# Forgetting attention with a dense MLP on one Trainium2 core: the weights' scale moves into the exponential's bias, and GpSimd takes the low parts of the first 512 keys

## The chip, the core and the metric

The kernel runs on one core of one Trainium2 chip. A core has five engines that work through queues of their own: TensorE (PE, matrix products; PEld is its weight load), VectorE (DVE), ScalarE (ACT), GpSimd (POOL) and SyncE (SP, which here only issues DMAs). The metric is the device time of one execution in microseconds; less is better.

## The reference, cut to what matters

One layer (`DEPTH = 1`): forgetting attention over 2048 frames with 16 heads of 64, then an MLP of width 4096.

```python
def fox_mixer(h, w_in, b_f, q_g, k_g, w_out):
    proj = h @ w_in
    q, k, v, f_pre = jnp.split(proj, [D, 2 * D, 3 * D], axis=-1)
    ...
    F = jnp.cumsum(log_f, axis=1).transpose(0, 2, 1)
    ...
        logits = (jnp.einsum('bqhd,bkhd->bhqk', q_i, k).astype(jnp.float32) * scale
                  + (F_i[..., :, None] - F[..., None, :]))
        logits = jnp.where(k_pos[None, :] <= q_pos[:, None], logits, -jnp.inf)
        p = jax.nn.softmax(logits, axis=-1).astype(v.dtype)
        return jnp.einsum('bhqk,bkhd->bqhd', p, v)
    ...
    return o @ w_out
```

The layer is `x = x + g_m * fox_mixer(h)` and then `x = x + g_f * (square(relu(h2 @ w_mlp_in)) @ w_mlp_out)`, with normed and shifted `h` and `h2`.

## The kernel before

Precision comes from pairs: a number is split into a high part in a short type and a low part, and products are summed over the pairs. Heads are taken two at a time, as 8 groups `g`. For a group, `sweeps` makes q, k and v of all frames (PE matmuls at L487 to L489 into `psq`, inputs split by ACT into `hh` at L406 and by GpSimd into `hl` at L407). The sweep of the next group is interleaved with `attention` of this one. Attention walks over 16 query blocks `i` of 128 rows, and in each over two heads `h`; what follows calls one (g, i, h) a head. There are 256 heads, and a head of block `i` has W = 128(i+1) keys.

For a head, in this order:

- `att_scores`: PE writes the logits into PSUM, 1024 keys at a time (`S`, two buffers, L537 to L540). One DVE instruction (L544) adds the forget term, writes `L` to SBUF and puts the row maximum of these 1024 keys into `mx`. L549 takes the larger of the one or two maxima and negates it into `st`.
- `att_exp`: ACT turns `L` into exp(L + st) in place, in fp32 (L555). Then, for each chunk of up to `PW` = 1024 keys, ACT writes the fp16 high part of 2^15 times `L` into the first half of a tile `ph` (L562). There are `NPH` = 4 tiles `ph`. Tiles of the same ring also hold `wa` (a weight block that DVE accumulates at L197 while groups 0 to 4 run) and `wv`.
- `att_transpose`: DVE writes the low part, 2^15 `L` minus the high part, into the second half of `ph` (L574). In the last group and from block 8 on, the last 256 keys of a chunk over 512 go to GpSimd, in two instructions (L578 scales, L579 subtracts). Then SP issues a DMA that transposes the whole `ph` into a tile `pT` (L582). There are `NPT` = 5 tiles `pT`.
- `att_values`: PE multiplies the transposed high and low parts with v (L600, L601) into `po`; DVE sums and GpSimd scales the output (L609, L611).

The calls are staggered: `att_transpose` of a head comes after the scores of the next, `att_values` two or three heads later. A scheduler then orders each engine's instructions, and a tile of a ring is taken again when its last reader is done, so a copy L562 can wait for a transpose four chunks back, and a transpose for the values five chunks back. SP runs its queue in order: transposes, loads of `hl` (L403), of `F` (L395), of weights, and stores. After attention comes the output projection with the MLP, which PE fills alone.

Of the kernel before, what the change touches and what calls it, by code (L numbers as in the profile page):

```python
# [4 lines left out]

# [1 line left out]

# [7 lines left out]
F32 = mybir.dt.float32  # L15
# [9 lines left out]
P = 128  # L25
# [12 lines left out]
EPS = 1e-6  # L38
MASK = -1.0e30
PSCALE = 32768.0  # L40
PW = 1024
NL, NPH, NPT, NK, NV, NQD = 3, 4, 5, 6, 7, 1
AHEAD, LEAD, LAG_S, LAG_L = 1, 0.7, 3, 2
# [6 lines left out]
NEARLY, EARLY0 = 5, 12  # L50
TAPER, LEAD1 = 6.6, 0.6
QSH, QDM = 0, 0
LEAD0, NORM_AT, ADA0, ADA1, NF = 0.5, 8, 60, 10, 5


# [2 lines left out]
def fox_layer(ctx, tc, x, c, norm_mix, norm_mlp, w_ada, b_ada, w_mlp_in, w_mlp_out,  # L58
# [77 lines left out]
    def pri(n):  # L136
        return tc.high_priority(offset=n)
# [37 lines left out]
    with ExitStack() as st:  # L175
# [161 lines left out]
        def value_scale(g):  # L337

            wv = sb.tile([P, KB, P], F32, tag="ph" if g else "k", name=f"wv{g}", bufs=NPH if g else NK)
            nc.sync.dma_start(wv, w_in[:, 2 * D + g * P:2 * D + (g + 1) * P].rearrange("(k p) c -> p k c", p=P))  # L340
            r = sb.tile([P, 2], F32, tag="lsr", name=f"lsr_w{g}", bufs=2)
            nc.scalar.activation(wv, wv, AF.Square, accum_out=r[:, 0:1])
            lw = sb.tile([P, 2], F32, tag="lw", name=f"lw{g}", bufs=2)
            log_sum(r, lw, f"w{g}")
            nc.vector.tensor_tensor(lw, lw, hs2, op=ALU.add)
            nc.scalar.activation(vsc[:, g:g + 1], lw[:, 0:1], AF.Exp, scale=-0.5)
            nc.vector.tensor_scalar(vsc[:, g:g + 1], vsc[:, g:g + 1], PSCALE, None, op0=ALU.mult)
            nc.vector.reciprocal(osc[:, g:g + 1], vsc[:, g:g + 1])
            nc.vector.tensor_scalar(osc[:, g:g + 1], osc[:, g:g + 1], 1.0 / PSCALE, None, op0=ALU.mult)

        kT, qT, vT, Fb = {}, {}, {}, {}
        carry = sb.tile([NH, 1], F32, tag="carry", name="carry", bufs=1)
# [169 lines left out]
        def att_scores(g, i, h, st, L):  # L522
# [6 lines left out]
            for cch in range(j + 1):  # L529
# [11 lines left out]
                if last or cch % 2 == 1:  # L541
                    c0, c1 = cch // 2 * 2 * TJ, cch * TJ + w
                    with pri(PR_T):
                        nc.vector.tensor_tensor_reduce(  # L544
                            out=L[:, c0:c1], in0=s2[:, :c1 - c0], in1=Fb[g, h, cch // 2][:, :c1 - c0],
                            scale=1.0, scalar=-3.0e38, op0=ALU.add, op1=ALU.max, accum_out=mx[:, cch // 2:cch // 2 + 1])
                yield
            with pri(PR_T):
                nc.vector.tensor_reduce(out=st[:, h:h + 1], in_=mx[:, :j // 2 + 1], axis=AX.X, op=ALU.max, negate=True)  # L549

        def att_exp(g, i, h, st, L):

# [12 lines left out]

        def att_transpose(g, i, h, L, phs):
            W = (i + 1) * P
            pts = []
            for n, ph in enumerate(phs):
                s0 = n * PW  # L570
                w = min(PW, W - s0)
                c = w - min(w, POOL_B * P) if i >= POOL_I and g >= POOL_G and w > TJ else w
                with pri(PR_PL):
# [7 lines left out]
                with pri(PR_DT):  # L581
                    nc.sync.dma_start_transpose(pT[:, :2 * w // P, :], ph[:, :2 * w])  # L582
                pts.append(pT)
            return pts

        po_of, n_po = {}, [0]
        po_all = psO.tile([P, 2, 2, P], F32, tag="O", name="po")
# [1 line left out]
        def att_values(g, i, h, st, pts):  # L589
# [4 lines left out]
            po = po_of[g, i]  # L594
            for b in range(nb):
                v = vT[g, b // RB][:, b % RB, h, :]
                pT, bb = pts[b * P // PW], b % (PW // P)
                nw = min(PW // P, nb - b + bb)
                with pri(PR_PO):
                    nc.tensor.matmul(po[:, h, :], lhsT=pT[:, bb, :], rhs=v, start=(b == 0), stop=False)  # L600
                    nc.tensor.matmul(po[:, h, 0:HD], lhsT=pT[:, nw + bb, :], rhs=v[:, 0:HD],  # L601
                                     start=False, stop=(b == nb - 1))
                if b % RB == RB - 1:
                    yield
# [342 lines left out]
```

## Time and profile before

| | |
|---|---|
| median of 3 runs | 3117.88 us (3115.86 to 3118.42) |
| the profiled execution | 3121.49 us, of which its instructions span 3119.8 us |
| busy over the span | PE 92%, PEld 76%, DVE 62%, ACT 46%, GpSimd 33% |
| mean granted TensorE clock | 0.966 |

Busy time is a share of the whole span. Attention takes the first 1490 us or so and the MLP the rest, and the shares of the two differ much; the rows below take them apart. An instruction's duration on DVE and GpSimd includes time in which it is held up after it has started.

### The profile page before, as it was taken

The numbers are of one execution on the slowest core, as the hardware profiler recorded it, in microseconds if no ns is written. First come the engines' busy times: TensorE is split into PE (matmuls) and PEld (weight loads), VectorE is DVE, ScalarE is ACT, GpSimd is POOL, SyncE is SP. The second block draws the span as 40 slices with busy tenths as digits, with TensorE's granted clock in tenths as the row PEclk, the third lists the DMA queues.
The fourth block names the chain that finished last, engine by engine and source line by source line (L and its number), as shares of the span: only waits on it lengthen the run. The fifth ranks groups of instructions, "written<-read, shape, count | busy, mean of one in ns | idle before, by whom it ended". The sixth has DMA issues, their size and how long they took to land.

```text
span 3119.8 us, 44614 instructions
## 1 busy us (share of the span) xinstructions
PE 2870.4 (92%) x16587; PEld 2375.9 (76%) x16587; DVE 1930.7 (62%) x3319; ACT 1433.1 (46%) x2267; POOL 1040.5 (33%) x811
## 2 busy tenths in 40 slices
PE   4788889888988898988999999999999999999999
PEld 4667777777877777776788888788887888878887
DVE  6688978988888877878356433443335333453334
ACT  4466766666676767766233322232222223222321
POOL 3354545545464645445332100410013001311103
PEclk9799989999999999998999999999999999999999
DMA  8479999999999989979755432543235323352332
GB/s 274 124 174 208 208 193 218 209 204 208 213 209 211 201 191 197 189 163 211 215 191 200 132 93 80 172 138 95 75 108 203 94 81 108 95 192 91 108 94 69
DMA packets 852122, 502.34 MB, mean 161 GB/s; under 512 B 585396, under 2 KB 782076, under 8 KB 851904
## 3 DMA queue, kind: packets, MB, share of 16 engines
q1 hardware_dynamic: 843536, 469.60, 62.1%
q0 software_dynamic: 8368, 29.89, 2.5%
q8 instruction: 130, 2.13, 0.3%
q14 instruction: 88, 0.72, 0.1%
HBM read 310.50 MB, written 46.28 MB: 114 GB/s over the span
## 4 chain that ended last, share of the span: by engine, by line
PE 49%; DVE 1%; DMA 1%; ACT 0%; issue 0%; SPq 0%; POOL 0%; DVEq 0%; ACTq 0%
PE my L134 8%; PE my L132 7%; PE my L133 7%; PE pu L134 7%; PE pu L132 7%; PE pu L133 7%; PE py L132 1%; PE py L133 1%; PE py L134 1%; DVE w L865 1%; DMA w1r<-in_w_mlp_in_dram 1%; PE xt L799 0%; PE e_py L132 0%; DMA pT<-ph 0%; PE e_py L134 0%; PE e_py L133 0%
## 5 line engine op out<-in xcount | busy, mean ns | idle before, releaser
L574 DVE SCALAR_TENSOR_TENSOR ph<-L,ph 128x1024 f16<-128x1024 f32 (+7 forms) x384 | 438.3, 1152 | 81.2 <-ACT ph L562 79.5
L887 POOL TENSOR_TENSOR rl<-rl 128x512 f32<-128x512 f32 x128 | 139.1, 1086 | 1024.6 <-ACT rl L886 1019.7
L864 ACT CAST w<-w1r 128x1024 fp32r<-128x1024 f32 x128 | 133.5, 1043 | 598.6 <-PE my L134 553.5
L132 PE MATMUL my<-w,a 128*128 128x512 f32 x1024 | 405.0, 396 | 0.1
L133 PE MATMUL my<-w,a 128*128 128x512 f32 x1024 | 402.9, 394 | 0.0
L134 PE MATMUL my<-w,a 128*128 128x512 f32 x1024 | 395.9, 396 | 2.9 <-DVE a L890 2.9
L562 ACT ACTIVATE ph<-L 128x1024 f16<-128x1024 f32 (+7 forms) x384 | 301.7, 804 | 177.4 <-DMA pT<-ph 152.6
L407 POOL TENSOR_TENSOR hl<-hl,hh 128x1024 fp32r<-128x1024 f32 x120 | 299.5, 2497 | 243.7 <-ACT hh L406 205.4
L487 PE MATMUL psq<-w,hh 128*128 128x384 f32 (+1 forms) x960 | 343.5, 359 | 26.5 <-DVE v L496 12.5
L489 PE MATMUL psq<-w,hl 128*128 128x384 f32 (+1 forms) x960 | 354.4, 371 | 3.2 <-POOL hl L407 2.9
L544 DVE CUSTOM_DVE_ANT_0 L<-S,F 128x1024 f32<-128x1024 f32 (+7 forms) x384 | 343.1, 904 | 19.5 <-PE S L538 6.7
L488 PE MATMUL psq<-w,hh 128*128 128x384 f32 (+1 forms) x960 | 342.7, 359 | 6.1 <-POOL w L333 6.1
L555 ACT ACTIVATE L<-L,st 128x128 f32<-128x128 f32 (+15 forms) x256 | 306.7, 1198 | 89.2 <-DVE st L549 84.9
L537 PE MATMUL S<-kT,qT 128*128 128x512 f32 (+3 forms) x640 | 261.8, 411 | 77.4 <-DVE mx L544 66.6
L600 PE MATMUL po<-v,pT 128*128 128x128 f16 x2176 | 277.1, 228 | 55.4 <-DMA pT<-ph 47.0
L865 DVE TENSOR_TENSOR w<-w1r,w 128x1024 fp32r<-128x1024 f32 x128 | 169.9, 1328 | 236.6 <-ACT w L864 236.6
L915 DVE TENSOR_TENSOR ya<-my,ya 128x512 f32<-128x512 f32 x192 | 128.0, 687 | 292.7 <-PE my L134 292.7
L134 PE MATMUL pu<-m_h,w 128*128 128x512 f32 x768 | 304.4, 396 | 0.0
L132 PE MATMUL pu<-m_h,w 128*128 128x512 f32 x768 | 303.8, 396 | 0.0
L133 PE MATMUL pu<-m_h,w 128*128 128x512 f32 x768 | 301.8, 393 | 0.0
L865 DVE TENSOR_TENSOR w<-w2r,w 128x1024 fp32r<-128x1024 f32 x128 | 165.7, 1295 | 203.7 <-ACT w L864 203.7
L600 PEld LDWEIGHTS <-pT 128*128 128x128 f16 x2176 | 205.1, 103 | 86.2 <-DMA pT<-ph 58.3
(214 smaller groups left out, 6115.8 us busy)
## 6 DMA issues: line engine op xcount, KB each, us to landing
w1r<-in_w_mlp_in_dram SPq DMA_DIRECT2D x128, 512.0 KB
w2r<-in_w_mlp_out_dram SPq DMA_DIRECT2D x128, 512.0 KB
hl<-hT_d SPq DMA_DIRECT2D x120, 512.0 KB
F<-nF_d SPq DMA_DIRECT2D x64, 256.0 KB
wa<-in_w_ada_dram SPq DMA_DIRECT2D x32, 512.0 KB
x<-in_x_dram SPq DMA_DIRECT2D x27, 512.0 KB
wr<-in_fox_w_in_dram SPq DMA_DIRECT2D x64, 192.0 KB
h_d<-h2r POOLq DMA_DIRECT2D x24, 512.0 KB, 3.4
```

Source lines behind the costliest of these rows:

```text
L132: nc.tensor.matmul(ps, lhsT=a[0], rhs=b[0], start=first, stop=False)
L133: nc.tensor.matmul(ps, lhsT=a[0], rhs=b[1], start=False, stop=False)
L134: nc.tensor.matmul(ps, lhsT=a[1], rhs=b[0], start=False, stop=last)
L487: nc.tensor.matmul(ps[:, :n], lhsT=hh, rhs=w[:, 0, :n], start=(kb == 0), stop=False)
L488: nc.tensor.matmul(ps[:, :n], lhsT=hh, rhs=w[:, 1, :n], start=False, stop=False)
L489: nc.tensor.matmul(ps[:, :n], lhsT=hl, rhs=w[:, 0, :n], start=False, stop=(kb == KB - 1))
L544: nc.vector.tensor_tensor_reduce(out=L[:, c0:c1], in0=s2[:, :c1 - c0], in1=Fb[g, h, cch // 2][:, :c1 - c0], scale=1.0, scalar=-3.0e38, op0 ...
L555: nc.scalar.activation(L[:, :W], L[:, :W], AF.Exp, bias=st[:, h:h + 1], scale=1.0, accum_out=st[:, 2 + h:3 + h])
L562: nc.scalar.activation(ph[:, :w], L[:, s0:s0 + w], AF.Copy, scale=PSCALE)
L574: nc.vector.scalar_tensor_tensor(ph[:, w:w + c], L[:, s0:s0 + c], PSCALE, ph[:, :c], op0=ALU.mult, op1=ALU.subtract)
L600: nc.tensor.matmul(po[:, h, :], lhsT=pT[:, bb, :], rhs=v, start=(b == 0), stop=False)
L865: nc.vector.tensor_tensor(w[:, 1, :], raw, w[:, 0, :].bitcast(F32), op=ALU.subtract)
```

## The change

The factor 2^15 goes from the copy and the subtraction into the exponential: the bias `st` is now -max + ln 2^15, so `L` itself comes out scaled, the high part is a plain copy, and the low part a plain subtraction. The sum of the row carries the factor too, so `osc` no longer divides by it. The second L544 of a head starts from the first one's maximum, and the last maximum is negated and shifted by a tensor_scalar in place of the reduction.

A function `plan` sets the chunks. Blocks 0 to 7 stay as they are. In blocks 8 to 15 the first 512 keys are a chunk of their own, whose low part GpSimd makes, in all groups; the rest follows in chunks of up to 1024 whose low part DVE makes. (In the last group GpSimd goes on to take the last 256 keys of a chunk over 512, now in one instruction.) So blocks 8 to 11 keep two chunks a head, and blocks 12 to 15 have three in place of two. The branch "pe" is not used.

```diff
+TURN_I, HEADS = 8, ("pool",)
...
-            nc.vector.tensor_scalar(osc[:, g:g + 1], osc[:, g:g + 1], 1.0 / PSCALE, None, op0=ALU.mult)
...
-                            scale=1.0, scalar=-3.0e38, op0=ALU.add, op1=ALU.max, accum_out=mx[:, cch // 2:cch // 2 + 1])
+                            scale=1.0, scalar=mx[:, 0:1] if cch > 1 else -3.0e38, op0=ALU.add, op1=ALU.max, accum_out=mx[:, cch // 2:cch // 2 + 1])
                 yield
             with pri(PR_T):
-                nc.vector.tensor_reduce(out=st[:, h:h + 1], in_=mx[:, :j // 2 + 1], axis=AX.X, op=ALU.max, negate=True)
+                nc.vector.tensor_scalar(st[:, h:h + 1], mx[:, j // 2:j // 2 + 1], -1.0, LN_PSCALE, op0=ALU.mult, op1=ALU.add)
+
+        def plan(i):
+
+            W = (i + 1) * P
+            if i < TURN_I:
+                return [(s0, min(PW, W - s0), "dma") for s0 in range(0, W, PW)]
+            head = [(k * TJ, TJ, how) for k, how in enumerate(HEADS)]
+            return head + [(s0, min(PW, W - s0), "dma") for s0 in range(len(head) * TJ, W, PW)]
...
-            for s0 in range(0, W, PW):
-                w = min(PW, W - s0)
+            for s0, w, how in plan(i):
...
-                    nc.scalar.activation(ph[:, :w], L[:, s0:s0 + w], AF.Copy, scale=PSCALE)
+                    nc.scalar.copy(ph[:, :w], L[:, s0:s0 + w])
...
-                    nc.vector.scalar_tensor_tensor(ph[:, w:w + c], L[:, s0:s0 + c], PSCALE, ph[:, :c],
-                                                   op0=ALU.mult, op1=ALU.subtract)
-                    if c < w:
-                        lt = L[:, s0 + c:s0 + w]
-                        nc.gpsimd.tensor_scalar(lt, lt, PSCALE, None, op0=ALU.mult)
-                        nc.gpsimd.tensor_tensor(ph[:, w + c:2 * w], lt, ph[:, c:w], op=ALU.subtract)
...
+                    c = w - min(w, POOL_B * P) if i >= POOL_I and g >= POOL_G and w > TJ else w
+                    c = 0 if how == "pool" else c
+                    with pri(PR_PL):
+                        if c > 0:
+                            nc.vector.tensor_tensor(ph[:, w:w + c], L[:, s0:s0 + c], ph[:, :c], op=ALU.subtract)
+                        if c < w:
+                            nc.gpsimd.tensor_tensor(ph[:, w + c:2 * w], L[:, s0 + c:s0 + w], ph[:, c:w], op=ALU.subtract)
+                    with pri(PR_DT):
+                        nc.sync.dma_start_transpose(pT[:, :2 * w // P, :], ph[:, :2 * w])
```

The scheduler orders anew. Three places in group 4 show it; in a name such as ph_12_0_512, 12 is the block, 0 the head and 512 the chunk's first key.

SP before, at block 12: two transposes a head, of 16 and of 10 blocks of 128 by 128 (high and low parts together).

```order
L582 DMA_TRANSPOSE pT_12_0_0_11122<-ph_12_0_0_11047 128x16x128
L613 DMA o_d_82<-ot_10_11105 128x128
L216 DMA gate_11212<-in_b_ada_dram 1x1024
L403 DMA hl_9_11336<-hT_d_66 128x1024
L325 DMA wr_3_12069<-in_fox_w_in_dram 128x3x128
L582 DMA_TRANSPOSE pT_12_0_1024_11125<-ph_12_0_1024_11049 128x10x128
L582 DMA_TRANSPOSE pT_12_1_0_11201<-ph_12_1_0_11128 128x16x128
L582 DMA_TRANSPOSE pT_12_1_1024_11204<-ph_12_1_1024_11130 128x10x128
```

SP now, at the same place: three a head, of 8, 16 and 2 blocks.

```order
L600 DMA_TRANSPOSE pT_12_0_0_11277<-ph_12_0_0_11201 128x8x128
L405 DMA hl_8_11344<-hT_d_66 128x1024
L630 DMA o_d_82<-ot_10_11261 128x128
L219 DMA gate_11378<-in_b_ada_dram 1x1024
L600 DMA_TRANSPOSE pT_12_0_512_11280<-ph_12_0_512_11203 128x16x128
L600 DMA_TRANSPOSE pT_12_0_1536_11283<-ph_12_0_1536_11205 128x2x128
L600 DMA_TRANSPOSE pT_12_1_0_11361<-ph_12_1_0_11287 128x8x128
L600 DMA_TRANSPOSE pT_12_1_512_11364<-ph_12_1_512_11289 128x16x128
L405 DMA hl_9_11506<-hT_d_66 128x1024
L630 DMA o_d_83<-ot_11_11446 128x128
L600 DMA_TRANSPOSE pT_12_1_1536_11367<-ph_12_1_1536_11291 128x2x128
```

The same blocks are moved by one more instruction a head, and the load hl_9 now stands behind four transposes that it stood ahead of.

ACT before, at block 12: exponentials of both heads, then the copies.

```order
L562 ACTIVATE ph_12_0_0_11047<-L_12_0_10966 128x1024
L555 ACTIVATE L_12_1_11051,st_12_10965<-L_12_1_11051,st_12_10965 128x1664
L406 CAST hh_7_11075<-hl_7_11073 128x1024
L494 COPY qk_1_10831<-psq_1_1_10972 128x256
L495 ACTIVATE v_1_10832<-psq_1_1_10972,vsc 128x2x64
L562 ACTIVATE ph_12_0_1024_11049<-L_12_0_10966 128x640
L562 ACTIVATE ph_12_1_0_11128<-L_12_1_11051 128x1024
L562 ACTIVATE ph_12_1_1024_11130<-L_12_1_11051 128x640
```

ACT now:

```order
L574 CAST ph_12_0_0_11201<-L_12_0_11120 128x512
L565 ACTIVATE L_12_1_11207,st_12_11119<-L_12_1_11207,st_12_11119 128x1664
L574 CAST ph_12_0_512_11203<-L_12_0_11120 128x1024
L574 CAST ph_12_0_1536_11205<-L_12_0_11120 128x128
L408 CAST hh_7_11231<-hl_7_11229 128x1024
L496 COPY qk_1_10985<-psq_1_1_11126 128x256
L497 ACTIVATE v_1_10986<-psq_1_1_11126,vsc 128x2x64
L574 CAST ph_12_1_0_11287<-L_12_1_11207 128x512
L565 ACTIVATE L_13_0_11294,st_13_11293<-L_13_0_11294,st_13_11293 128x1792
L574 CAST ph_12_1_512_11289<-L_12_1_11207 128x1024
```

Three copies a head, each with a tile of the same ring of four; the sweep's `hh`, `qk` and `v` now stand behind the third copy of the head.

GpSimd now, at block 12 (before, the same row held the sweep's and the output's instructions alone):

```order
L409 TENSOR_TENSOR hl_6_11121<-hl_6_11121,hh_6_11123 128x1024
L598 TENSOR_TENSOR ph_12_0_0_11201<-L_12_0_11120,ph_12_0_0_11201 128x512
L431 TENSOR_TENSOR qn_0_11018<-qk_0_10482,y_q_0_10974 128x1024
L628 TENSOR_TENSOR ot_10_11261<-ot_10_11261,st_10_10818 128x128
L409 TENSOR_TENSOR hl_7_11229<-hl_7_11229,hh_7_11231 128x1024
L598 TENSOR_TENSOR ph_12_1_0_11287<-L_12_1_11207,ph_12_1_0_11287 128x512
```

One subtraction a head stands among the sweep's and the output's instructions, and in this queue each waits its turn behind the one ahead.

## Rows read from the trace of the kernel before

**Rows 1.** Stages: stretch, PE, PEld, DVE, ACT, POOL busy, PEclk, DMA share, GB/s.
```profile
200.00:1480.00 1280.00, 1114.85 (x8724) 954.45 (x8724) 1086.94 (x2132) 875.86 (x1457) 667.79 (x500) 0.94 0.98 202
1500.00:3119.00 1619.00, 1610.68 (x7069) 1296.80 (x7067) 698.39 (x827) 455.81 (x610) 292.81 (x243) 1.00 0.38 125
```

**Rows 2.** Waits from 200 to 1480: us in total, times, longest us.
```profile
ACT ph L562 <- DMA pT<-ph: 148.5, 100, 6.4
DVE ph L574 <- ACT ph L562: 74.9, 75, 3.6
...
PE S L537 <- DVE mx L544: 64.1, 50, 4.7
...
PE po L600 <- DMA pT<-ph: 37.4, 31, 3.1
...
PE psq L487 <- DVE v L496: 12.5, 7, 4.4
...
PE po L600 <- DVE ot L609: 8.2, 9, 3.3
```

**Rows 3.** Subtractions on DVE, both inputs in SBUF, in the MLP: min/median/max ns.
```profile
L804 DVE TENSOR_TENSOR h2r<-h,h2r x32: 683/693/1673, 1552.1 to 1735.3; 128x512 fp32r<-128x512 f32 x32
...
L865 DVE TENSOR_TENSOR w<-w2r,w x128: 1210/1218/3434, 1671.1 to 3075.4; 128x1024 fp32r<-128x1024 f32 x128
```

**Rows 4.** Low parts on DVE, stretch 200 to 1480: busy us, mean ns, idle before.
```profile
L574 DVE SCALAR_TENSOR_TENSOR ph<-L,ph 128x1024 f16<-128x1024 f32 x142 | 209.8, 1481 | 36.3 <-ACT ph L562 35.3
...
L574 DVE SCALAR_TENSOR_TENSOR ph<-L,ph 128x512 f16<-128x512 f32 x32 | 37.6, 1174 | 2.8 <-ACT ph L562 2.7
```

**Rows 5.** GpSimd: a subtraction of 512, and the last group's pair: min/median/max ns.
```profile
L887 POOL TENSOR_TENSOR rl<-rl x128: 1031/1040/2046, 1682.2 to 3093.2; 128x512 f32<-128x512 f32 x128
...
L578 POOL TENSOR_SCALAR L<-L x24: 846/1224/1639, 1391.4 to 1487.7; 128x256 f32<-128x256 f32 x24
...
L579 POOL TENSOR_TENSOR ph<-L,ph x24: 667/674/1690, 1392.4 to 1491.7; 128x256 f16<-128x256 f32 x24
```

**Rows 6.** Exponentials at 1010 us: group 5 begins where the width falls to 128.
```profile
L555 ACT ACTIVATE L<-L,st x2: 398/398/398, 1010.7 to 1011.0; 128x128 f32<-128x128 f32 x2
```

**Rows 7.** Groups 2 to 4 and groups 5 and 6, columns as in rows 1.
```profile
502.00:1011.00 509.00, 441.39 (x3426) 381.20 (x3425) 440.59 (x837) 346.27 (x589) 266.50 (x191) 0.94 1.01 209
1011.00:1326.00 315.00, 281.39 (x2252) 241.97 (x2250) 260.21 (x522) 225.37 (x378) 167.32 (x126) 0.95 0.96 194
```

**Rows 8.** L197 alone in groups 2 to 4: DVE busy, PEclk, DMA share, GB/s.
```profile
502.00:1011.00 509.00, 35.88 (x20) 0.94 1.01 209
```

**Rows 9.** Transposes on SP: ns from start to end, min/median/max.
```profile
L582 SPq DMA_TRANSPOSE pT<-ph x384: 1167/1853/6677, 120.1 to 1496.2; - x192
```

**Rows 10.** Copies on ACT by width, up to 1800 us: busy us, mean ns.
```profile
L562 ACT ACTIVATE ph<-L 128x1024 f16<-128x1024 f32 x160 | 168.1, 1055 | 80.1 <-DMA pT<-ph 76.8 <-DVE acc L197 1.9 <-issue 0.4
...
L562 ACT ACTIVATE ph<-L 128x512 f16<-128x512 f32 x32 | 19.8, 623 | 6.4 <-DMA pT<-ph 6.3
```

**Rows 11.** DVE and GpSimd in order of time: start us, us, instruction.
```profile
906.21 1.98 POOL L333 TENSOR_TENSOR w<-wr,w 128x384 fp32r<-128x384 f32 x2
906.25 1.01 DVE L121 TENSOR_SCALAR v_q<-ssq 128x16 f32<-128x16 f32 x1
...
907.25 2.02 DVE L574 SCALAR_TENSOR_TENSOR ph<-L,ph 128x1024 f16<-128x1024 f32 x1
```

**Rows 12.** Small DVE instructions: min/median/max ns; the last row busy us, mean ns.
```profile
L549 DVE TENSOR_REDUCE st<-mx x256: 125/144/156, 115.6 to 1477.0; 128x1 f32<-128x1 f32 x64, 128x1 f32<-128x2 f32 x64
...
L349 DVE TENSOR_SCALAR osc<-osc x8: 134/151/155, 61.7 to 1159.6; 128x1 f32<-128x1 f32 x8
...
L121 DVE TENSOR_SCALAR v_q<-ssq x32: 146/168/2324, 84.1 to 1389.9; 128x16 f32<-128x16 f32 x32
...
L121 DVE TENSOR_SCALAR v_q<-ssq 128x16 f32<-128x16 f32 x32 | 10.9, 340 | 0.1
```

**Rows 13.** The chain that ended last, near attention's end: start us, us.
```profile
1478.23 1.62 POOL L L578
```

More of the change, by code (lines that the diff above doesn't have):

```diff
@@ L8 @@
+import math
 from contextlib import ExitStack
@@ L40 @@
 PSCALE = 32768.0
+LN_PSCALE = math.log(PSCALE)
 PW = 1024
@@ L557, in att_exp @@
             phs = []
-            for s0 in range(0, W, PW):
-                w = min(PW, W - s0)
+            for s0, w, how in plan(i):
+                if how == "pe":
+                    phs.append(None)
+                    continue
                 ph = sb.tile([P, 2 * PW], F16, tag="ph", name=f"ph{g}_{i}_{h}_{s0}", bufs=NPH)
                 with pri(PR_E):
-                    nc.scalar.activation(ph[:, :w], L[:, s0:s0 + w], AF.Copy, scale=PSCALE)
+                    nc.scalar.copy(ph[:, :w], L[:, s0:s0 + w])
                 phs.append(ph)
@@ L566, in att_transpose @@
         def att_transpose(g, i, h, L, phs):
[L567 to L573, printed above, removed]
-                    nc.vector.scalar_tensor_tensor(ph[:, w:w + c], L[:, s0:s0 + c], PSCALE, ph[:, :c],
-                                                   op0=ALU.mult, op1=ALU.subtract)
-                    if c < w:
-                        lt = L[:, s0 + c:s0 + w]
-                        nc.gpsimd.tensor_scalar(lt, lt, PSCALE, None, op0=ALU.mult)
-                        nc.gpsimd.tensor_tensor(ph[:, w + c:2 * w], lt, ph[:, c:w], op=ALU.subtract)
-                pT = sb.tile([P, 2 * PW // P, P], F16, tag="pT", name=f"pT{g}_{i}_{h}_{s0}", bufs=NPT)
-                with pri(PR_DT):
-                    nc.sync.dma_start_transpose(pT[:, :2 * w // P, :], ph[:, :2 * w])
-                pts.append(pT)
@@ L584, in att_transpose @@
-            return pts
+            by_block = []
+            for (s0, w, how), ph in zip(plan(i), phs):
+                n = w // P
+                pT = sb.tile([P, 2 * PW // P, P], F16, tag="pT", name=f"pT{g}_{i}_{h}_{s0}", bufs=NPT)
+                if how == "pe":
+                    pt = psT.tile([P, TJ], F32, tag="T", name=f"pp{g}_{i}_{h}")
+                    for b in range(n):
+                        nc.tensor.transpose(pt[:, blk[b]], L[:, s0 + b * P:s0 + (b + 1) * P], ident)
+                    hi, lo = [pT[:, k * n:(k + 1) * n, :].rearrange("p b c -> p (b c)") for k in range(2)]
+                    nc.scalar.copy(hi, pt)
+                    nc.vector.tensor_tensor(lo, pt, hi, op=ALU.subtract)
+                else:
+                    c = w - min(w, POOL_B * P) if i >= POOL_I and g >= POOL_G and w > TJ else w
[7 more added lines that the diff above has]
+                        nc.sync.dma_start_transpose(pT[:, :2 * w // P, :], ph[:, :2 * w])
+                by_block += [(pT[:, b, :], pT[:, n + b, :]) for b in range(n)]
@@ L586, in fox_layer @@
+            return by_block
         po_of, n_po = {}, [0]
@@ L596, in att_values @@
                 v = vT[g, b // RB][:, b % RB, h, :]
-                pT, bb = pts[b * P // PW], b % (PW // P)
-                nw = min(PW // P, nb - b + bb)
+                p_hi, p_lo = pts[b]
                 with pri(PR_PO):
-                    nc.tensor.matmul(po[:, h, :], lhsT=pT[:, bb, :], rhs=v, start=(b == 0), stop=False)
-                    nc.tensor.matmul(po[:, h, 0:HD], lhsT=pT[:, nw + bb, :], rhs=v[:, 0:HD],
+                    nc.tensor.matmul(po[:, h, :], lhsT=p_hi, rhs=v, start=(b == 0), stop=False)
+                    nc.tensor.matmul(po[:, h, 0:HD], lhsT=p_lo, rhs=v[:, 0:HD],
                                      start=False, stop=(b == nb - 1))
```

## The prediction

> **What bounds the kernel now.** I read the stages first [rows 1]. From 200 to 1480 us attention runs with the sweeps. PE is busy 1115 of 1280 us, DVE 1087, the DMA engines have a share of 0.98, ACT 876, GpSimd 668. After 1500 us PE is busy 1611 of 1619 us. The change has no instruction there, so that half should keep its length, and whatever comes must come out of the 165 us in which PE idles in attention. None of PE, DVE and the DMA engines has much room there, which is why no single engine's busy time can be turned into a gain.
>
> Next, who waits for whom in that stretch [rows 2]. PE waits 64.1 us for DVE's maximum to give back a PSUM buffer of scores, 12.5 us for v and 8.2 us for the output sum, both DVE's too: 84.8 us, half of the 165. It waits 37.4 us for transposed weights. Behind it stands another wait: ACT waits 148.5 us for a `ph` tile that a transpose still reads, and DVE 74.9 us for ACT's copies. So DVE is late partly from its own work and partly because tiles come back late. The change eases the first and strains the second.
>
> **DVE sheds work.** The low parts drop from 384 instructions to 320. In groups 0 to 6, 112 heads lose 512 keys each. In the last group, where GpSimd already had 256 keys of each chunk over 512, eight heads lose 512 and eight lose 256. Together that is 124 times 512 keys. A subtraction on DVE with both inputs in SBUF takes 683 ns for 512 and 1210 ns for 1024 when nothing holds it up [rows 3]: 527 ns for 512 elements, 156 ns fixed. So 124 x 0.527 = 65.4 us, and the 64 instructions that vanish (the second chunk of a head in blocks 8 to 11 merges into one of 640 to 1024 keys) give 64 x 0.156 = 10.0 us. DVE sheds 75.4 us. Today's instructions have a mean of 1481 ns for 1024 and 1174 ns for 512 [rows 4], far over those prices; the excess is waiting, costed below.
>
> **GpSimd gains work.** It gets 128 subtractions of 512, at 1.04 us by the nearest row [rows 5] 133 us. In the last group its 24 scalings of 1.22 us go (29 us) and its 24 subtractions of 256 become 16 (8 x 0.67 = 5 us). Net +99 us, from 668 to 767 of 1280, so it has room. A subtraction may stand behind a 1024-wide instruction of the sweep, but SP works on the other chunks meanwhile only if they stand ahead of it, and the first chunk's transpose stands first. I count nothing for it here; it goes into the third chunk's price.
>
> **Copies, tiles and transposes.** Blocks 0 to 11 keep their number. In blocks 12 to 15, 64 heads get a third chunk: a third copy, a third tile out of four `ph` and out of five `pT`, a third transpose, while the transposed bytes stay. On ACT a copy takes 1055 ns for 1024 and 623 ns for 512 [rows 10], so 191 ns fixed: 64 x 0.19 = 12 us. Its present wait for tiles is 148.5 us over 384 copies, 0.39 us each [rows 2]; 64 more at that rate wait 25 us. On SP a transpose occupies the queue for at least 1.167 us [rows 9], 75 us for 64. I take ACT's 37 us as the load, and nothing for SP, since a long transpose holds the queue up to 6.7 us today and the moved bytes are equal; the end with SP's 75 us shown in full is kept for the range.
>
> **Small edits.** The reduction that ends a maximum takes 144 ns, a tensor_scalar on one element 151 ns [rows 12]: nothing. The second L544 now needs the first one's maximum. Its price isn't in the trace; it lies between nothing and one small instruction each, 128 x 0.15 = 19 us of DVE. I take nothing, since the accumulator's read already stands between the two on DVE. Dropping the factor from the exponential's side and eight tiny instructions on `osc` is worth about 1 us and left out.
>
> **Port.** DVE and GpSimd hold each other up [rows 11]: GpSimd ran two subtractions from 906.21 to 908.19, and a low part of 1024 that DVE started at 907.25 took 2.02 us instead of 1.21, ending 1.08 us after GpSimd was done. So the work handed over comes back in part as waiting. Today the 1024-wide low part waits 1481 - 1210 = 271 ns on average, over 384 instructions at most 104 us, with GpSimd busy 52% of the stretch. With 320 instructions and GpSimd at 60% it is 0.271 x 60/52 x 320 = 100 us. Fewer instructions and a busier neighbour cancel, and I count nothing. The other end: at the prices above today's low parts (532 times 512 keys) are 384 x 0.156 + 532 x 0.527 = 340 us and 104 us of waiting, 35% of the stretch, so 35% of the 99 us, 34 us, could be added.
>
> The Trainium skill, "SBUF — State Buffer", section "Who interferes with whom", speaks against this change: a DVE instruction with two SBUF inputs contends with a GpSimd instruction that reads SBUF, and one of the two is blocked for the other's whole length; it adds that a tensor_scalar can contend too and a tensor_reduce never. By that rule the new subtractions cost DVE waits, and so may the tensor_scalar that replaces the reduction. The trace agrees on the first [rows 11]. On the second it is split [rows 12]: on 16 elements a tensor_scalar went up to 2324 ns, on one element it never passed 155 ns in 8 instances. The sum by the rule is the fourth rival's.
>
> **From engine time to the end.** How much of DVE's time reaches PE? An upper bound comes from the kernel itself. Groups 2 to 4 take 509/3 = 169.7 us each, groups 5 and 6 315/2 = 157.5 us [rows 6, 7], 12.2 us less. What differs is L197, 35.9 us of DVE in three groups, 12.0 us each [rows 8]: a ratio of 1.0. But with it go its weight loads (DMA share 1.01 against 0.96) and `ph` tiles, so 1.0 is the top. The bottom is 0, if transposes set the pace. I take 0.5, the share of PE's idle time that names DVE (84.8 of 165).
>
> **The sum**, against the profiled execution's 3121.5 us: DVE -75.4 x 0.5 = -37.7; third chunk +37 x 0.5 = +18.5; the scaling L578, which stands once in the last chain at attention's end [rows 13], -1.6. Net -20.8, so 3100.7. The median of the runs shown lies 3.6 us below the profiled execution, so I predict **3097 us**. With the ratio between 0.35 and 0.65 for DVE this case spans 3086 to 3108.
>
> **Rivals**, each as a median.
>
> - *DVE sets the pace outright.* Ratio 1.0 on what it sheds: -75.4 + 18.5 - 1.6 = -58.5, 3059 us. For it: PE's largest wait names DVE. Against: PE idles only 165 us in all, and the DMA engines are as full as DVE.
> - *The third chunk costs more than DVE sheds: slower.* The place is blocks 12 to 15, the four `ph` tiles and SP's queue. It decides once a head there loses over (37.7 + 1.6)/64 = 0.61 us. With SP's 1.17 us as the most and 0.9 us as the middle of the two: 64 x 0.9 - 39.3 = +18, 3136 us. For it: the 148.5 us that ACT already waits for tiles; `hl` loads stand behind more transposes. Against: PE itself waits only 37.4 us for transposes, and blocks 8 to 11 have the gain without this cost.
> - *The gain is hidden: the DMA engines set the pace.* Their share is 0.98 and their bytes don't change, so DVE finishes earlier and waits. 3116 us with the 1.6 us of the end. Against: PE's wait for DVE is over twice that for transposes.
> - *The shared port eats it.* With 34 us more waiting, DVE sheds 41 us: -20.7 + 18.5 - 1.6 = -3.8, 3114 us, no change that shows. If the one-element tensor_scalar is held up as the 16-element one is, by 340 - 168 = 172 ns on average [rows 12], 256 of them add 44 us and DVE ends 3 us fuller than before: +1.3 + 18.5 - 1.6 = +18, 3136 us. The page named above would have both.
>
> **Chances.** A measurement of this kernel tells about 0.2% (6 us) from no change. My forecast 0.47 and DVE's pace 0.10 make faster 0.57. Hidden 0.10 and the port alone 0.08 make no change 0.18. The third chunk 0.20 and the port with the tensor_scalar 0.05 make slower 0.25. The range from 3058 to 3137 leaves out the further half of the first and the second rival, 0.15.
>
> **What would show it.** Low parts on DVE at 320 instructions and some 75 us less busy; PE's wait for DVE's maximum from 64 towards 40 us; attention's end some 20 us earlier and the MLP's length unchanged. ACT's wait for `ph` tiles should grow, in blocks 12 to 15. If groups with blocks 12 to 15 get longer while blocks 8 to 11 get shorter, the third chunk's price is what I mis-sized. If a one-element tensor_scalar reaches 300 ns on average, the port's rule holds there. The forecast is wrong if PE's idle time in attention doesn't fall, or if the granted clock there moves from 0.94 by more than 0.02, which I took as fixed.

## The result and the profile after

The changed kernel took 3147.64 us (median of 4 runs, 3145.49 to 3152.51) against 3118.15 before: a ratio of 1.0098, interval 1.008 to 1.0115. It is slower by 29.5 us where 3097 us were forecast.

The stages of the changed kernel come first, columns as in [rows 1].

```profile
200.00:1510.00 1310.00, 1128.67 (x8740) 951.39 (x8739) 1032.89 (x2063) 885.42 (x1518) 775.65 (x605) 0.94 0.97 197
1530.00:3147.00 1617.00, 1605.12 (x7033) 1292.85 (x7031) 695.91 (x826) 455.19 (x609) 290.49 (x238) 1.00 0.38 124
```

Behind the last value matmul, at 1511.9 us before and 1545.2 us now, 1607.9 and 1602.2 us are left: the second half is no longer than it was. The loss lies in attention, which ends 33 us later, though VectorE has become less busy and GpSimd busier, as the change wants. Its waits, from 200 to 1480 us as in [rows 2]:

```profile
ACT ph L574 <- DMA pT<-ph: 164.9, 128, 5.7
...
POOL ph L598 <- ACT ph L574: 122.9, 54, 6.8
DVE ph L596 <- ACT ph L574: 97.2, 99, 4.1
...
PE S L539 <- DVE mx L546: 71.1, 67, 3.4
PE po L617 <- DMA pT<-ph: 58.3, 58, 4.0
```

(The stretch leaves out the last 65 us of attention here and the last 32 us in the kernel before.) PE's wait for DVE's maximum did not fall from 64.1 us; it is 71.1. Its wait for transposed weights rose from 37.4 to 58.3 us, and the copies' wait for a `ph` tile from 148.5 to 164.9 us. The low parts on DVE and on GpSimd, DVE's new small instruction, and the transposes on SP (min/median/max ns):

```profile
L596 DVE TENSOR_TENSOR ph<-L,ph 128x1024 f16<-128x1024 f32 (+7 forms) x320 | 354.5, 1112 | 115.1 <-ACT ph L574 112.7
...
L598 POOL TENSOR_TENSOR ph<-L,ph x144: 666/1167/2155, 214.1 to 1527.9; 128x512 f16<-128x512 f32 x128, 128x256 f16<-128x256 f32 x16
...
L551 DVE TENSOR_SCALAR st<-mx x256: 122/145/158, 115.1 to 1509.5; 128x1 f32<-128x1 f32 x128
...
L600 SPq DMA_TRANSPOSE pT<-ph x448: 1167/1438/5795, 119.5 to 1534.7; - x150
```

The same group of DVE in the kernel before, over the whole run:

```profile
L574 DVE SCALAR_TENSOR_TENSOR ph<-L,ph 128x1024 f16<-128x1024 f32 (+7 forms) x384 | 438.3, 1152 | 81.2 <-ACT ph L562 79.5
```

So DVE shed 438.3 - 354.5 = 83.8 us of low parts, even more than the 75.4 forecast, and none of it reached the end. By the starts of the exponentials, groups 0 to 6 spend 351 us in blocks 8 to 11 (372 before) and 441 us in blocks 12 to 15 (399 before). This split is rough, since the sweeps that run beside a block shift too, but it points at the blocks with a third chunk, and it is the sign that the prediction named for a third chunk whose price was mis-sized.

### The profile page after: what moved, and what is told of

It reads as the page before. It is cut to its first block, busy times and chain, and to the rows that moved or that the text cites. A ratio compares the mean times of both kernels' runs of the same rounds, so it can differ in the third digit from the quotient of the medians.

```text
span 3147.4 us, 45107 instructions
## 1 busy us (share of the span) xinstructions
PE 2881.7 (92%) x16587; PEld 2371.5 (75%) x16587; DVE 1875.0 (60%) x3247; ACT 1444.5 (46%) x2331; POOL 1143.7 (36%) x907
## 4 chain that ended last, share of the span: by engine, by line
PE 48%; DMA 2%; DVE 1%; issue 1%; POOL 1%; ACT 1%; SPq 0%; POOLq 0%; ACTq 0%; DVEq 0%
PE my L137 8%; PE my L135 7%; PE my L136 7%; PE pu L137 7%; PE pu L135 7%; PE pu L136 7%; PE py L136 1%; PE py L137 1%; PE py L135 1%; DVE w L882 1%; DMA pT<-ph 1%; DMA w1r<-in_w_mlp_in_dram 1%; POOL ph L598 0%; PE xt L816 0%; SPq L600 0%
## 5 line engine op out<-in xcount | busy, mean ns | idle before, releaser
L596 DVE TENSOR_TENSOR ph<-L,ph 128x1024 f16<-128x1024 f32 (+7 forms) x320 | 354.5, 1112 | 115.1 <-ACT ph L574 112.7
L574 ACT CAST ph<-L 128x512 f16<-128x512 f32 (+4 forms) x448 | 311.5, 708 | 218.0 <-DMA pT<-ph 183.0
L617 PE MATMUL po<-v,pT 128*128 128x128 f16 x2176 | 283.7, 228 | 84.8 <-DMA pT<-ph 72.8
L546 DVE CUSTOM_DVE_ANT_0 L<-S,F 128x1024 f32<-128x1024 f32 (+7 forms) x256 | 251.8, 985 | 24.1 <-PE S L540 8.3
```

Of the source, the lines that this page charges most:

```text
L574: nc.scalar.copy(ph[:, :w], L[:, s0:s0 + w])
L596: nc.vector.tensor_tensor(ph[:, w:w + c], L[:, s0:s0 + c], ph[:, :c], op=ALU.subtract)
L617: nc.tensor.matmul(po[:, h, :], lhsT=p_hi, rhs=v, start=(b == 0), stop=False)
```

## The experiments

Each was timed against the kernel before on the same chip, which took 3118.3 to 3120.3 us there. A time is a median, and its ratio to the kernel before, with the 95% interval, stands behind it.

### First: the parts of the change apart

**Two chunks in blocks 12 to 15**; GpSimd takes the first 512 keys inside the first chunk's tile.

```diff
-            if i < TURN_I:
-                return [(s0, min(PW, W - s0), "dma") for s0 in range(0, W, PW)]
+            if i < TURN_I or i >= 12:
+                return [(s0, min(PW, W - s0), "half" if i >= 12 and s0 == 0 else "dma") for s0 in range(0, W, PW)]
...
+                        b0 = TJ if how == "half" else 0
+                        if b0:
+                            nc.gpsimd.tensor_tensor(ph[:, w:w + b0], L[:, s0:s0 + b0], ph[:, :b0], op=ALU.subtract)
...
+                            nc.vector.tensor_tensor(ph[:, w + b0:w + c], L[:, s0 + b0:s0 + c], ph[:, b0:c], op=ALU.subtract)
```

> The changed kernel, except that blocks 12 to 15 keep two chunks a head (1024 and the rest, as before the change): GpSimd takes the low parts of the first 512 keys of the first chunk, DVE those of the other 512, in one tile. GpSimd's and DVE's work is the changed kernel's; the third copy, tile and transpose are gone. Third-chunk theory: both the gain of blocks 8 to 11 (30 us) and one in blocks 12 to 15 remain, 3065 to 3095 us. Handover theory (GpSimd's subtractions and the shared port cost the time): 3140 us or more. If the order of the instructions is all: anything between.

Measured: 3098.66 us, 0.9931 (0.9911 to 0.9951), 4 us above the range of the third-chunk theory.

**The third chunk alone**: 512, 1024 and the rest in blocks 12 to 15, all low parts on DVE, blocks 0 to 11 as before.

```diff
-            if i < TURN_I:
+            if i < 12:
...
-            head = [(k * TJ, TJ, how) for k, how in enumerate(HEADS)]
-            return head + [(s0, min(PW, W - s0), "dma") for s0 in range(len(head) * TJ, W, PW)]
+            return [(0, TJ, "dma")] + [(s0, min(PW, W - s0), "dma") for s0 in range(TJ, W, PW)]
```

> The third chunk alone: blocks 12 to 15 are cut into 512, 1024 and the rest as in the changed kernel, but DVE makes all low parts (the last group's last 256 keys of a chunk over 512 aside), and blocks 0 to 11 have the chunks of before. Third-chunk theory: the loss without the gain, 3150 to 3180 us. Handover theory: within 8 us of the 3118 us of before.

Measured: 3150.69 us, 1.0094 (1.0074 to 1.0114).

**Blocks 8 to 11 alone**; blocks 12 to 15 as before.

```diff
-            if i < TURN_I:
+            if i < TURN_I or i >= 12:
```

> GpSimd takes the first 512 keys in blocks 8 to 11 alone; blocks 12 to 15 have the two chunks of before with DVE's low parts. Third-chunk theory: the gain of blocks 8 to 11 alone, 3085 to 3100 us. Handover theory: half of the handovers, so about half of the loss, 3125 to 3140 us.

Measured: 3094.70 us, 0.9914 (0.989 to 0.9939), the fastest version of this study.

**The scale alone.**

```diff
-TURN_I, HEADS = 8, ("pool",)
+TURN_I, HEADS = 16, ("pool",)
```

> The scale in the exponential's bias alone, with the maximum's small instructions and the last group's single subtraction on GpSimd; chunks and low parts as before. Both theories: 3108 to 3122 us. Over 3125 us would say that the small edits (the tensor_scalar, the chained maximum) cost time.

Measured: 3119.29 us, 1.0 (0.9988 to 1.0012).

The third chunk alone is slower by as much as the whole change. Without it the change is faster: 3147.64 - 3098.66 = 49 us over 64 heads, 0.77 us each, past the 0.61 us at which its rival decides. The scale, the chained maximum and the one-element tensor_scalar cost nothing that shows.

### Second: what helps in blocks 8 to 11, and the third chunk's tiles

**The cut alone**: 512 and the rest in blocks 8 to 11, both on DVE.

```diff
-            if i < TURN_I:
+            if i < TURN_I or i >= 12:
...
-                    c = 0 if how == "pool" else c
```

> The run in which GpSimd helps in blocks 8 to 11 alone (3095 us), but DVE makes the low parts of the 512 chunk there too: the cut into 512 and 640 to 1024 without the handover. If the handover makes the gain: 3114 to 3122 us. If the cut makes it (evener chunks): 3092 to 3102 us.

Measured: 3112.41 us, 0.9981 (0.9969 to 0.9993), between the ranges of the two theories.

**The handover alone**: blocks 8 to 11 keep 1024 and the rest, and GpSimd takes the first 512 keys inside the first tile, with the code of the first experiment.

```diff
-            if i < TURN_I:
-                return [(s0, min(PW, W - s0), "dma") for s0 in range(0, W, PW)]
+            if True:
+                return [(s0, min(PW, W - s0), "half" if 8 <= i < 12 and s0 == 0 else "dma") for s0 in range(0, W, PW)]
```

> The handover without the cut: blocks 8 to 11 keep 1024 and the rest as before, and GpSimd takes the low parts of the first 512 keys inside the 1024 chunk; blocks 12 to 15 as before. If the handover makes the gain: 3092 to 3104 us. If the cut makes it: 3114 to 3122 us.

Measured: 3120.20 us, 1.0000 (0.9989 to 1.0011): neither half alone makes the gain. The low parts on DVE, and those of 512 keys among them:

```profile
L599 DVE TENSOR_TENSOR ph<-L,ph 128x512 f16<-128x512 f32 (+7 forms) x384 | 429.6, 1129 | 64.1 <-ACT ph L574 62.5
```

```profile
L599 DVE TENSOR_TENSOR ph<-L,ph 128x512 f16<-128x512 f32 x98 | 108.8, 1111 | 23.4 <-ACT ph L574 22.8
```

At 0.527 us for each of 64 times 512 keys, 33.7 us were handed over; DVE's low parts fell by 438.3 - 429.6 = 8.7 us, or by 15.8 against the 445.4 us of the run with the scale alone, which has the same plain subtractions. The rest came back as longer instructions: 512 keys took 1111 ns on average, against 683 to 693 ns where nothing holds a subtraction up [rows 3]. This agrees with the Trainium skill, "SBUF — State Buffer", section "Who interferes with whom", by which a DVE instruction with two SBUF inputs contends with a GpSimd instruction that reads SBUF; that this is the whole reason no run shows. In the whole change the work did not come back.

**The third chunk with a shared `ph` tile**, and **with a shared `pT` tile**: the last chunk takes the free half of the first one's.

```diff
-                ph = sb.tile([P, 2 * PW], F16, tag="ph", name=f"ph{g}_{i}_{h}_{s0}", bufs=NPH)
+                if i >= 12 and s0 == TJ + PW:
+                    ph = phs[0][:, 2 * TJ:]
+                else:
+                    ph = sb.tile([P, 2 * PW], F16, tag="ph", name=f"ph{g}_{i}_{h}_{s0}", bufs=NPH)
```

> The third chunk alone (3151 us), but the first and the third chunk of a head lie in one ph tile, so a head takes two of the four again; it still takes three pT tiles, three copies and three transposes. If the ph ring is the price: 3115 to 3130 us. If the pT ring, SP or ACT is: 3142 to 3160 us.

Measured: 3141.16 us, 1.0071 (1.0048 to 1.0094).

> The third chunk alone (3151 us), but the first and the third chunk of a head lie in one pT tile, so a head takes two of the five again; it still takes three ph tiles, three copies and three transposes. If the pT ring is the price: 3115 to 3130 us. If the ph ring, SP or ACT is: 3142 to 3160 us.

Measured: 3152.71 us, 1.0108 (1.0088 to 1.0128). The third chunk alone had cost 31 us; a shared `ph` gives back some 10 of them, a shared `pT` nothing.

### Third: tiles, instructions or the transpose

**Both tiles shared** (the two edits above together).

> The third-chunk run (512, 1024 and the rest in query blocks 12 to 15, VectorE making all low parts), with the first and the last chunk laid into one ph tile and one pT tile, so that a head takes two tiles of each kind, as before. Sharing ph alone gave 10 us back of the 31, sharing pT alone nothing. Theory that the third chunk costs tiles (four ph and five pT in all): with both shared the time falls to the kernel before's, 3115 to 3125 us. Theory that it costs a third transpose on the queue: the three transposes are still there, so no lower than the shared-ph run, 3135 to 3145 us. Theory that it costs the extra instructions of ScalarE (64 copies of some 0.2 us of fixed cost) and VectorE: also 3135 to 3145 us.

Measured: 3143.06 us, 1.0074 (1.0057 to 1.0091).

**One transpose for the first and the last chunk**, everything else as in the run before it:

```diff
+            if i >= 12:
+                t = W - TJ - PW
+                tiles = [(phs[0], [(0, TJ), (TJ + PW, t)]), (phs[1], [(TJ, PW)])]
...
+                with pri(PR_DT):
+                    nc.sync.dma_start_transpose(pT[:, :2 * n, :], ph[:, :2 * tw])
```

> As the run that shares both tiles, but one DMA transpose moves the first and the last chunk together (three copies and three subtractions a head as in the third-chunk run, two transposes a head as before). Theory of the third transpose: 3115 to 3125 us, and at least 12 us below the run that shares both tiles with three transposes. Theory of tiles: equal to that run within 5 us, both at 3115 to 3125. Theory of the extra instructions on ScalarE and VectorE: equal to that run within 5 us, both at 3135 to 3145.

Measured: 3113.47 us, 0.9979 (0.9967 to 0.999).

**The whole second chunk for GpSimd in blocks 12 to 15**, with blocks 8 to 11 as in the fastest version.

```diff
+                return [(s0, min(PW, W - s0), "pool" if s0 and i >= 12 else "dma") for s0 in range(0, W, PW)]
```

> The run with GpSimd's 512-key chunk in query blocks 8 to 11 alone (3094.7 us), and in blocks 12 to 15, where it keeps the two chunks of before, GpSimd subtracts the whole of the second (640 to 1024 keys), VectorE the whole of the first. Theory that what helps is a chunk of GpSimd's own beside VectorE's, with no chunk more than before: another 10 to 25 us, 3070 to 3085 us. Rival, that GpSimd's pace decides (by its 1.25 us for 512 keys an estimate of 1.5 to 2.5 us for such a chunk, against VectorE's 0.7 to 1.2 us for the same widths) and the second chunk's transpose comes later than before: no gain or a loss, 3095 to 3130 us. Rival that VectorE's load decides: 64 subtractions of about 1 us leave VectorE, half of that is 30 us, 3065 us.

Measured: 3102.73 us, 0.9957 (0.994 to 0.9974): the theory missed, and the rival of GpSimd's pace had the range. DVE's low parts fell to 316.0 us, the lowest of all, and the kernel is 8 us slower than without it.

The two runs before this one decide: 64 transposes fewer, with all three copies and subtractions in place, give 3143.06 - 3113.47 = 29.6 us, 0.46 us each. The instructions on ACT and DVE were not the price, and the tiles were worth 3150.69 - 3143.06 = 8 of the 31 us. In the change itself:

**The whole change with one transpose for the first and the last chunk.**

> The whole change (GpSimd makes the low part of the first 512 keys in all of query blocks 8 to 15), only that in blocks 12 to 15 the first and the last chunk lie in one ph tile and one pT tile and one DMA transpose moves both, two transposes a head as before instead of three. Theory that the third transpose is what made the change slower: the 28 to 35 us that it cost in the runs without GpSimd's share come back and the gain of blocks 8 to 11 (25 us) shows, so 3085 to 3105 us against 3148. Rival, that GpSimd's 512 columns in blocks 12 to 15 are late by themselves (1.25 us each, after a copy that waits for a tile): 3110 to 3125 us. Rival that with GpSimd's share another thing than the transpose holds these blocks: above 3135 us.

Measured: 3107.87 us, 0.9965 (0.9954 to 0.9976): 39.8 us below the change as it stands, 0.62 us for each of 64 transposes and the tiles that went with them, and faster than the kernel before. It lies 3 us above the theory's range, and 9 us above the version with two chunks.

### Fourth: is it the number of transposes, and whose time is it

**64 transposes more in the kernel before** (blocks 12 to 15), and **128 more** (blocks 8 to 15): the first chunk's in two halves.

```diff
+                    if i >= 12 and n == 0:
+                        nc.sync.dma_start_transpose(pT[:, w // P:2 * w // P, :], ph[:, w:2 * w])
+                        nc.sync.dma_start_transpose(pT[:, :w // P, :], ph[:, :w])
```

> The kernel before (two chunks, two copies, two subtractions a head), only that in query blocks 12 to 15 the transpose of the first chunk is issued as two, one for the low parts and one for the high parts: 64 transposes more, the same bytes and tiles. Theory that each transpose has a price of its own on the queue, whatever it carries (0.46 us from three transposes against two with all else equal): 64 x 0.46 = 29 us, 3140 to 3155 us. Rival, that the price was that of a later chunk (its copy and its subtraction come last, and the merge took that off): no chunk comes later here, 3112 to 3126 us.

Measured: 3125.24 us, 1.0022 (1.0013 to 1.0031), within the rival's range.

> As the run with 64 transposes more, in query blocks 8 to 15: 128 more than before. Theory of a price for each transpose: 128 x 0.46 = 59 us, 3165 to 3195 us, about twice the loss of the run with 64. Rival that the queue has room and only the time at which a chunk is ready counts: 3112 to 3126 us. If the loss is the same as with 64 more, the price is one of blocks 12 to 15 and not of the transposes' number.

Measured: 3142.16 us, 1.007 (1.0053 to 1.0087). This lies between what the theory and its rival expected. The number of transposes alone costs 6 and 23 us, 0.10 and 0.18 us each, not the 0.46 us of the third chunk's.

**Copies that nothing reads**, large and small, behind each store of a block's output (the edit of the large ones):

```diff
+                nc.sync.dma_start(dram.tile([P, (g + 1) * P], F32, name=f"spare{g}_{i}"), o_d[i][:, :(g + 1) * P])
```

> The kernel before with 128 copies that nothing reads, from DRAM to DRAM, one behind each store of a block's attention output: 64 KB to 512 KB each, 37.7 MB in all. Theory that the DMA engines' work bounds the attention stage (busy 0.96 of 1397 us, at 199 GB/s): the copies take 60 to 180 us of the engines, at most 56 us of that fits into their idle time, so 3150 to 3250 us, with the DMA share at 0.97 or more. Rival, that the chain of copy, subtraction, transpose and matmul bounds it and the DMA engines only look busy: within 10 us of the run with small copies.

Measured: 3214.51 us, 1.0303 (1.0279 to 1.0327).

> The same 128 copies in the same places, of 2 KB each. What the issue and the wait for the store on the queue cost without the bytes: 3118 to 3135 us by both theories; the difference to the large copies is the engines' work.

Measured: 3169.56 us, 1.0162 (1.0137 to 1.0188), outside both theories' 3118 to 3135: 128 copies with next to no bytes cost 49 us. Not all of that is the price of an entry. A copy reads what the store ahead of it wrote, so SP stands until that store has landed, and its wait is

```profile
SPq L614 <- DMA o_d<-ot: 35.6, 30, 3.4
```

beside some 0.58 us at the median for which each copy itself holds SP. The 37.7 MB of the large ones come on top with 3214.51 - 3169.56 = 45 us.

**No transposes of low parts in blocks 12 to 15.**

```diff
+                    if half:
+                        nc.sync.dma_start_transpose(pT[:, :w // P, :], ph[:, :w])
...
+                    nc.tensor.matmul(po[:, h, 0:HD], lhsT=pT[:, bb if i >= 12 else nw + bb, :], rhs=v[:, 0:HD],
```

> The kernel before, only that in query blocks 12 to 15 the low parts are made but not transposed (their matmuls read the high parts in their place, as many as before), so that 58 of the 136 blocks' worth of transposed bytes is halved, a fifth of all. Theory of the DMA engines' work: 100 to 180 us of it go and the stage shortens until TensorE (1207 us busy) or VectorE is next, 2990 to 3060 us. Theory that the chain of small instructions and tiles sets the pace: the copies and subtractions are all there, 3090 to 3120 us.

Measured: 3093.50 us, 0.9914 (0.9886 to 0.9941): a gain of 27 us, the size that the theory of the small instructions and tiles expected, not the 60 us or more of the engines' work.

What the DMA engines did shows in the stretch from 115 us to the last value matmul, with the columns of [rows 1]. The kernel before:

```profile
115.00:1511.90 1396.90, 1206.85 (x9302) 1031.73 (x9303) 1158.60 (x2324) 931.05 (x1564) 717.25 (x540) 0.93 0.96 199
```

The large copies, the small copies, and the run without those low transposes:

```profile
115.00:1607.90 1492.90, 1238.62 (x9299) 1045.98 (x9299) 1150.75 (x2318) 936.55 (x1559) 707.99 (x543) 0.91 0.99 211
```

```profile
115.00:1554.80 1439.80, 1207.21 (x9284) 1024.25 (x9285) 1171.58 (x2325) 935.72 (x1564) 717.66 (x540) 0.93 0.94 193
```

```profile
115.00:1481.20 1366.20, 1180.19 (x9267) 1025.52 (x9267) 1185.17 (x2321) 929.51 (x1563) 718.51 (x538) 0.94 0.85 181
```

Length times share is taken as the engines' work, and the remainder as what they idle. (This is rough: a share sums the times of packets and can pass 1.00, as in [rows 7].) Before: 1341 us of work, 56 us idle. With small copies: 1353 and 86. With large ones: 1478 and 15. The bytes first fill the idle time, then lengthen the stage, so with the engines full, at a share of 0.99, they bind it. Without the low transposes the work is 1161 us, 180 us less, and the stage only 30.7 us shorter: another limit stands right behind. Which one is open; PE's wait for DVE's maximum rose there from 66.6 to 84.6 us over the stage.

**Three transposes a head, the third with no wait of its own**: the merged one cut so that its second part carries the last 1 to 3 low blocks.

```diff
+                    if len(parts) == 2 and i >= 13:
+                        cut = n + RB + 1
+                        nc.sync.dma_start_transpose(pT[:, :cut, :], ph[:, :cut * P])
+                        nc.sync.dma_start_transpose(pT[:, cut:2 * n, :], ph[:, cut * P:2 * tw])
```

> The run with one transpose for the first and the last chunk (3113 us), only that in query blocks 13 to 15 this transpose is issued as two, the second of them over the last 1 to 3 low blocks (48 transposes more, of which each head has three again). All that the second needs is there when the first may go, so that it waits for no instruction of its own. Theory of the transposes' number or of small transposes: 48 x 0.46 = 22 us, 3130 to 3142 us. Theory that it is an entry with its own wait in the queue that costs: 48 x 0.11 = 5 us, as with the 64 split transposes, 3110 to 3123 us.

Measured: 3166.55 us, 1.015 (1.0131 to 1.0169): 53.1 us above the merged run for 48 transposes, 1.1 us each. Both theories fall, that of the wait by the most. The small second parts on SP, then the stage:

```profile
L606 SPq DMA_TRANSPOSE pT<-ph x48: 1119/1247/2821, 290.8 to 1541.7; - x48
```

```profile
115.00:1554.80 1439.80, 1224.30 (x9284) 1033.44 (x9285) 1178.92 (x2380) 937.20 (x1628) 685.06 (x508) 0.92 0.93 193
```

And of the 64 split transposes (8 blocks each), one half's row:

```profile
L583 SPq DMA_TRANSPOSE pT<-ph x64: 1231/1281/4115, 274.7 to 1491.8; - x64
```

One to three blocks hold SP as long as eight: 1.25 against 1.28 us at the median. For the merged run the stage reads:

```profile
115.00:1491.60 1376.60, 1191.67 (x9284) 1015.65 (x9284) 1168.62 (x2377) 938.13 (x1626) 669.67 (x507) 0.94 0.97 202
```

The work is 1335 us there and 1339 in the cut run, the idle time 41 and 101 us: with the small transposes added, the DMA engines had no more to do and stood longer. (The merged run's profiled execution took 3105.13 us, 8 less than its median, so some 8 of these 60 us are scatter.)

## Why the prediction was wrong

**What bounds the kernel.** The share of 0.98 in [rows 1] was read as one engine among three without room, and the queue that feeds the DMA engines got no price. The runs show that this queue counts: more bytes and more small transposes both lengthen the stage. They don't show that it is the only limit, since 180 us less of the engines' work shortened it by 31. For the change itself the stage reads:

```profile
115.00:1545.20 1430.20, 1223.46 (x9323) 1031.02 (x9323) 1104.57 (x2253) 942.37 (x1627) 821.66 (x639) 0.93 0.95 195
```

PE idles 207 us there and 190 before, where the prediction had it fall; the granted clock is 0.93 in both. The DMA engines have 1359 us of work and 72 us idle, against 1341 and 56. The fastest version, blocks 8 to 11 alone, has 1327 and 41:

```profile
115.00:1483.50 1368.50, 1187.68 (x9283) 1009.51 (x9283) 1117.40 (x2248) 929.95 (x1562) 774.41 (x580) 0.94 0.97 203
```

The work hardly differs among these kernels, which move the same bytes (1327 to 1359 us; the share's last digit is worth 7 us either way), so the longer stage goes with engines that stand longer. That is bookkeeping and no cause: PE's column does the same (busy 1188 to 1224 us, idle 181 to 207). Two runs don't follow it, the 128 transposes more and the handover alone:

```profile
115.00:1537.40 1422.40, 1207.15 (x9318) 1027.14 (x9318) 1172.20 (x2320) 933.28 (x1561) 716.72 (x543) 0.93 0.96 196
```

```profile
115.00:1504.60 1389.60, 1192.07 (x9284) 1011.50 (x9285) 1166.25 (x2316) 931.39 (x1564) 762.23 (x572) 0.94 0.95 200
```

The first idles 57 us, as the kernel before, and is 25 us longer; the second idles 69 us and is no longer.

**Third chunk, +18.5: the term that failed.** It measured +31 us alone, +40 in the change for the transpose that it adds and the tiles shared with it, and +49 against the version with two chunks there. Of the 50.5 us by which the forecast missed, 49 - 18.5 = 30 are this term's, and most of the rest is the gain's, of which 21 us came in place of 37.7. The prediction put 37 us of load on ACT and halved them, and "nothing for SP". Most of the load sits in the place that was set at nothing, the transposes: the merged transpose gave 29.6 us back while ACT's copies stayed. The tiles' wait that the term was worked out from was worth 8 to 10 us. The reason given, that a long transpose holds the queue anyway and the bytes are equal, did not hold: 48 small ones cost 53 us with the bytes equal. The rival named the right blocks and the right queue and decided on the right side; its 3136 us was too low by 12 us, not for its price (64 x 0.9 = 58 us, against 49 measured) but for the gain that it set against it: 39 us, where the version with two chunks won 21.

An account that was formed from these runs, with estimates throughout: a transpose took SP at least 1.12 us even with 1 to 3 blocks, and a block of 128 x 128 is 180/928 = 0.19 us of the DMA engines' work (58 blocks in each of 16 heads left out). By these two numbers the engines would run dry while SP issues a transpose of fewer than some six blocks. The third chunk's last part has 2, 4, 6 and 8 blocks in blocks 12 to 15; with 1.17 us for an issue, the first two leave 0.78 and 0.39 us open, 0.29 us on average, 19 us for 64. The cut run's 1, 2 and 3 blocks leave 0.98, 0.78 and 0.59 us, 38 us for 48; the halves of 8 blocks leave nothing, and 128 small copies of 0.58 us at most 74 us. Measured: 30 to 40, 53, 6 (23 for 128) and 49. The order fits; the sizes are off by up to a factor of two, and the 23 us of the 128 halves are not in it at all. The cut in blocks 8 to 11 removes the same four small parts, by this account for 19 us, and won 7. Against it stands that a transpose of the change lands 4.8 us after its issue at the median, so that several are on their way at once and one short one need not let the engines run dry. A second account is SP's own time. Summed over the traces, the transposes hold SP for 926 us in the cut run against 873 in the merged one, 53 us for a loss of 53, and for 886 us in the change against 848 in its merged version, 38 us for 40; but against the kernel before (879 us) the change adds 7 us and loses 29.5. Neither was tried by itself, and every edit also made the scheduler order the queues anew, which no run holds fixed. So what makes a small transpose dear stays open; that the third one is dear is shown.

**DVE sheds 75.4 us, at 0.5: the size was right, the conversion was not.** Low parts on DVE and the time against before, run by run: 449.4 us and -7 (cut), 429.6 and 0 (handover), 376.6 and -12 (change, merged transpose), 375.3 and -25 (blocks 8 to 11), 375.0 and -21 (two chunks), 354.5 and +29 (the change), 316.0 and -16 (second chunk on GpSimd). There is no ratio in this, though the runs differ in more than DVE's load. In blocks 12 to 15 handing over gave nothing at all: -21 with it against -25 without. Reading 0.5 from PE's waits by the engine that they name was the mistake: a wait that names DVE ended with DVE, which says nothing on what made DVE late, and in the change this wait grew from 64.1 to 71.1 us while DVE's low parts shrank by 83.8. What gave the 25 us in blocks 8 to 11 needs both the cut (7 us alone) and the handover (0 alone); the rest of it is not explained.

**GpSimd, the port and the small edits.** A low part of 512 took 1.17 us at the median, not 1.04; no run shows that this moved the time. The port's rule held where both engines worked on one tile, and not as a loss in the whole change. The two-chunk run and the change with the merged transpose, where both work on one tile in blocks 12 to 15, have 375.0 and 376.6 us of low parts on DVE, no less than the 375.3 us of blocks 8 to 11 alone, though 60 times 512 keys more were handed over; with the tiles apart, in the change, they are 354.5 us. The one-element tensor_scalar was not held up in 256 instances (158 ns at most). The scale was worth nothing, as taken. The attention's end, -1.6, can't be told apart.

**The rival of the DMA engines** looked at the right place and had the wrong conclusion: it had the gain hidden, when the third transpose also cost time.

## What to carry to other kernels

Where the DMA engines' share is near 1.0 in a stage, price a change by what it adds to the queue that feeds them: the number of entries and the size of each, even when the bytes stay. Where a cut into more chunks leaves a small one, merge it with a neighbour in one tile and one transfer, as here, where that gave 30 and 40 us. And a wait's named engine is no conversion factor: one run that moves only that engine's load (the handover alone here) tells more than all the waits.

## What was unexpected of the hardware

The same matmuls of the stage took TensorE 1191.67 us at a mean granted clock of 0.94 in the merged run and 1238.62 us at 0.91 with the large copies. Of these two runs the one whose PE idles more (254 against 185 us) was granted less clock, so part of a loss shows as busy time, and a busy engine's sum is no constant to compare against. And a transpose of 1 to 3 blocks held SP as long as one of 8, 1.25 against 1.28 us, and 48 of them cost 53 us, where 64 of 8 blocks cost 6.
